# Sums of the input kept in DRAM, and weight sums moved between stages, in a two-layer trunk kernel

## Chip, cores and metric

The kernel runs on one core of a Trainium2 chip. The metric is the device time of one execution in microseconds (us), as the median of several runs. The engines are named as in the profile: PE (TensorE matmul), PEld (its weight loads), DVE (VectorE), ACT (ScalarE), POOL (GpSimd) and SP (SyncE, which here only issues transfers).

## The reference

One sequence of 512 tokens with 2048 channels passes two layers. In the first, `x @ w_in` gives q, k, v, a gate, `z` (1024 columns) and the inputs of a state-space scan. Attention and scan outputs are gated, the scan's by silu(z), concatenated and sent through a first output projection. The second is a pooling mixer: two projections `v` and `g`, causal window means, a small map per group, then `y @ w_out`, the second output projection. Each layer ends in `layer_norm(alpha * x + mixer(x))`.

```python
y = y.reshape(bsz, s, SSM_WIDTH) * jax.nn.silu(z.astype(F32))
...
return jnp.concatenate([y_att, y_ssm], axis=-1) @ w_out     # layer 1
...
return y @ w_out                                            # layer 2
```

## The kernel before

**Products.** All of it is fp32, as three fp32r matmuls per product (`mm3`, lines 105 to 107): each operand is cast to a high part on ACT (line 115) and the rest is taken on DVE (line 116); `split` does both. Weights come in units of 128x1024 (512 KB): `unit` loads one through SP's queue (line 122) into `raw`, and splits it into `hi` and `lo`; each of these three has three buffers. Units are scheduled ahead of other work.

**Winograd-like products.** z and the two output projections are made as 2x2 block products with seven multiplications in place of eight. They need sums of blocks of the activations and sums of blocks of the weights. For z the activation blocks are quarters of x: x1, x2 are the two halves of the channels, H0 and H1 the two halves of the tokens. z needs z1 = x1H1 - x2H1, z2 = z1 - x1H0, z3 = x1H0 - x1H1, z4 = z2 + x2H0. In the kernel before they are made in z's stage: `x_tile` loads 128x256 pieces of x from DRAM (line 511), DVE subtracts and adds piece by piece (lines 521, 535, 536, 538, 546), and each piece is split. The seven products are Yz, Vz (raw x), Wz, then Zz with z1, Yz with z2, Zz with z4, Yz with z3; each is 48 matmuls of 512 columns. The results go through `z_gate` into y.

**Weight sums.** `presum` makes the sums of weight blocks by DMA alone: it loads a block into an SBUF tile, loads others on top with an accumulating transfer, and writes the results t1 to t4 to DRAM, where `unit` fetches them later (`raw<-t`). All its transfers are issued on POOL's queue. One call is a "unit of sums" here: six loads and four writes, in seven steps separated by `yield`. z needs 4 units of sums (`wz`), the first output projection 8 (`wo1`), the second 8 (`wo2`).

**Lanes.** Side work is traced by generators in lanes. Each `mm3` ticks every lane by its nominal time (0.64 for 512 columns), and a lane traces its next step when the amount it yielded has passed. The two lanes `sums2` hold the units of sums, every second unit each; the pace was 7.0 per step. Lanes only set the order of the program: on the chip POOL takes its instructions in order as fast as their own waits let it. From the first `power` on (a small POOL operation that waits for DVE, line 230), `back` puts every transfer of the sums behind the last `power` traced. The pre tiles `pre0`, `pre30`, `pre1`, `pre31` in the pool `keep` are reused, after the lanes are flushed, by the tiles `sr` of the first output projection (line 748).

**Layer 2.** Four groups g of 512 channels: v blocks, g blocks, group map, and `yr[g]` written by ACT (line 960). A residual lane writes x1 to DRAM through POOL (line 905), and after group 0 POOL issues three transfers into `out` (line 965). The prefetch `xq` (line 979) waits on POOL for the last g block.

Of the kernel before, what the change touches and what calls it, by code (L numbers as in the profile page):

```python
# [8 lines left out]
F32 = mybir.dt.float32  # L9
# [17 lines left out]
GROUPS = (346, 346, 348)  # L27
WINDOWS = (2, 4, 8, 16)
NEG = -3.0e38
PACE = 7.0  # L30
AHEAD = 1000


# [22 lines left out]
class Lane:  # L56


    def __init__(self):
        self.gens, self.wait = [], 0.0  # L60

    def push(self, gen):
        if not self.gens:
# [7 lines left out]
            self.gens.pop(0)  # L71

    def tick(self, us):
        self.wait -= us
        while self.gens and self.wait <= 0:
            self.step()
# [6 lines left out]
def ts(j):  # L83
    return slice(j * P, (j + 1) * P)
# [3 lines left out]
def hybrid_trunk(ctx: ExitStack, tc: tile.TileContext, xT, xtok, wa, wg, wz, wo1, wo2, prm, con, lnp, out, dbg=None):  # L88
# [25 lines left out]
    def split(hi, lo, src):  # L114
        nc.scalar.copy(hi, src)  # L115
        nc.vector.tensor_tensor(lo, src, hi.bitcast(F32), ALU.subtract)  # L116
# [80 lines left out]
    def pair(tag):  # L197
        if tag == "sc":
            b = bank2("pZ2")
            return [b[:, 0], b[:, 1]]  # L200
        return [bank(tag, "pY" if tag == "mm" else "pZ") for _ in range(2)]
# [34 lines left out]
            else:  # L236
                nc.gpsimd.dma_start(dst, src)  # L237

    def presum(w, tsum, cp, ch, pool, n, after=None):

        def to(n, t):
            d = tsum[n, cp, ch] = dram.tile([P, 1024], F32, name=f"t{n}_{cp}{ch}")
            back(d, t)

        t = pool.tile([P, 1024], F32, tag=f"pre{n}", name="pre")
        t3 = pool.tile([P, 1024], F32, tag=f"pre3{n}", name="pre3")
        if after is not None:

            nc.gpsimd.tensor_copy(t[:, :1], after)
            nc.gpsimd.tensor_copy(t3[:, :1], after)  # L250
        back(t, wsrc(w, 0, 0, cp, ch))
        back(t3, wsrc(w, 0, 1, cp, ch))
        yield PACE
        back(t, wsrc(w, 0, 1, cp, ch), True)
        back(t3, wsrc(w, 1, 1, cp, ch), True)
        yield PACE
        to(1, t)
        to(3, t3)
        yield PACE
        back(t, wsrc(w, 1, 1, cp, ch), True)  # L260
        yield PACE
        to(2, t)
        yield PACE
        back(t, wsrc(w, 1, 0, cp, ch), True)
        yield PACE
        to(4, t)
        yield PACE


    with ExitStack() as l1:  # L270
# [14 lines left out]
        with ExitStack() as sd:  # L285
# [44 lines left out]
                            mm3(pts[i], hi[:, c], lo[:, c], xh[k], xl[k], k == 0, k == KT - 1)  # L330
            with tc.issue_after(last.ins):
                parameters()
            v = keep.tile([P, NT, 1024], F32, tag="v", name="v")
            y = keep.tile([P, NT, 1024], F32, tag="y", name="y")
            for i in range(4):
                conv_silu(bc[i], pts[i], 8 + i)
            bT, cT = bc[:2], bc[2:]
            btok = [sp.tile([P, 3, P], F32, name=f"btok{g}") for g in range(2)]
            cbm = [sp.tile([P, NT, P], F32, name=f"cbm{g}") for g in range(2)]
# [13 lines left out]
                    yield 3.0  # L353

            lane.push(bc_steps())
            for w, tsum, n in ((wz, tsz, 4), (wo1, ts1, 8), (wo2, ts2, 8)):
                for i in range(n):
                    sums2[i % 2].push(presum(w, tsum, i // 4, i % 4, keep, i % 2,
                                             bc[0][:, :1] if w is wz and i < 2 else None))


# [126 lines left out]
            def z_gate(t, j, c, th):  # L488
# [3 lines left out]
                yz = y[:, t, j * 512:(j + 1) * 512]  # L492
                nc.vector.tensor_tensor(yz, yz, th, ALU.mult)

            Yz, Vz = pair("mm"), pair("mm")
            for ch in range(4):
                prod(Yz, xblock(0, H0), unit(wsrc(wz, 0, 0, 0, ch)), ch, True, False)
# [4 lines left out]
        with tc.tile_pool(name="zs", bufs=1) as zq:  # L502
            def zsum(name):
                hi, lo = (zq.tile([P, 8, 256], F32R, tag=f"{name}{p}", name=f"{name}{p}") for p in "hl")
                return [hi[:, u] for u in range(8)], [lo[:, u] for u in range(8)]

            def x_tile(i, k, c):

                t = zq.tile([P, 256], F32, tag=f"x{i}", name=f"x{i}", bufs=2 + (i == 0))
                o = k % 2 * T + c.start  # L510
                nc.sync.dma_start(t, xT[k // 2 + 4 * (i % 2)][:, o:o + 256])
                return t

            def z_th():
                return zq.tile([P, T], F32, tag="zth", name="zth")

            Wz = pair("sc")
            z1, z2, z4 = zsum("z1"), zsum("z2"), zsum("z4")
            for k in range(8):
                a, b = x_tile(0, k, H1), x_tile(1, k, H1)  # L520
                nc.vector.tensor_tensor(a, a, b, ALU.subtract)
                split(z1[0][k], z1[1][k], a)
            for i in range(2):
                c = zq.tile([P, T], F32, tag="zc", name="zc")
                nc.scalar.copy(c, Yz[i])
                nc.vector.tensor_tensor(c, c, Vz[i], ALU.add)
                z_gate(i, 0, c, z_th())
            for ch in range(4):
                prod(Wz, xblock(8, H1), unit(tsz[4, 0, ch]), ch, True, True)
            Zz = pair("mm")  # L530
            for ch in range(4):
                prod(Zz, z1, unit(tsz[1, 0, ch]), ch, True, False)
            for k in range(8):
                d, e = x_tile(2, k, H0), x_tile(3, k, H0)
                nc.vector.tensor_tensor(d, z1[0][k], d, ALU.subtract)
                nc.vector.tensor_tensor(d, d, z1[1][k], ALU.add)
                split(z2[0][k], z2[1][k], d)
                nc.vector.tensor_tensor(e, e, d, ALU.add)
                split(z4[0][k], z4[1][k], e)
            z3 = zsum("z1")  # L540
            c22 = [zq.tile([P, T], F32, tag=f"c22{i}", name=f"c22{i}") for i in range(2)]
            for i in range(2):
                nc.scalar.copy(c22[i], Zz[i])
            for k in range(8):
                a, d = x_tile(0, k, H1), x_tile(2, k, H0)
                nc.vector.tensor_tensor(a, d, a, ALU.subtract)
                split(z3[0][k], z3[1][k], a)
            for ch in range(4):
                prod(Yz, z2, unit(tsz[2, 0, ch]), ch, False, False)
            for ch in range(4):  # L550
                prod(Zz, z4, unit(wsrc(wz, 1, 1, 0, ch)), ch, False, True)

            for i in range(2):
                c = zq.tile([P, T], F32, tag="zc", name="zc")
                nc.scalar.copy(c, Zz[i])
                nc.vector.tensor_tensor(c, c, Yz[i], ALU.subtract)
                z_gate(i, 1, c, z_th())
            for ch in range(4):
                prod(Yz, z3, unit(tsz[3, 0, ch]), ch, False, True)
            for i in range(2):  # L560
                c = zq.tile([P, T], F32, tag="zc", name="zc")
                nc.scalar.copy(c, Wz[i])
                nc.vector.tensor_tensor(c, c, Yz[i], ALU.add)
                z_gate(2 + i, 0, c, z_th())
                nc.vector.tensor_tensor(c22[i], c22[i], Yz[i], ALU.subtract)
                z_gate(2 + i, 1, c22[i], z_th())

        at = l1.enter_context(tc.tile_pool(name="att1", bufs=1))
        a2s = ExitStack()
# [292 lines left out]
    with ExitStack() as l2:  # L862
# [27 lines left out]
        with ExitStack() as mix:  # L890
# [18 lines left out]
            for g, w in enumerate(WINDOWS):  # L909
# [20 lines left out]
                if g == 0:  # L930
                    for c in range(4):
                        vblock(v0[:, c], vu[c], 256, T)
                        pool_block(c, v0[:, c], 0)
                    for c in range(4):
                        gblock(gts[:, c], gu[c], 0, T)
                else:
                    vu = [next_units(2) for _ in range(4)]
                    gu = [next_units(2) for _ in range(4)]
                    gts = lp.tile([P, 4, T], F32, tag="h2", name="gt")
                    for c in range(4):  # L940
                        vp = p2.tile([P, T + 16], F32, tag="vp", name="vp")
                        nc.vector.memset(vp[:, :16], 0.0)
                        vblock(vp[:, 16:], vu[c], 0, T)
                        pool_block(c, vp, 16)
                    for c in range(4):
                        gblock(gts[:, c], gu[c], 0, T)
                yr.append(lp.tile([P, 2, 2, T], F32, tag=("h0", "l0", "h1", "l1")[g], name=f"yr{g}"))
                for u in range(2):
                    hi, lo = unit(next_units(1)[0])
# [11 lines left out]
                if g == 0:  # L961
                    lane.flush()
                    with tc.issue_after(spill[-1].ins):
                        for t in (0, 2, 3):
                            nc.gpsimd.dma_start(out[0, ts(t)], lnp[1, 1].partition_broadcast(P))
                    a11 = (oc.tile([P, 8, 256], F32R, tag="xp0", name="a11h"), oc.tile([P, 8, 256], F32R, tag="xp1", name="a11l"))
                    s1 = (oc.tile([P, 8, 256], F32R, tag="xp2", name="s1h"), oc.tile([P, 8, 256], F32R, tag="xp3", name="s1l"))
                    sraw = lp.tile([P, 8, 256], F32, tag="l2", name="sraw")
# [214 lines left out]
```

## Time and profile before

| | |
|---|---|
| median of 3 runs | 1426.27 us (1425.15 to 1428.51) |
| the profiled execution | 1426.02 us, span 1424.3 us |
| PE busy | 1386.2 us (97%) |
| PEld busy | 1161.0 us (82%) |
| DVE busy | 878.3 us (62%) |
| ACT busy | 594.4 us (42%) |
| POOL busy | 186.2 us (13%) |
| DMA | 302.74 MB, mean 213 GB/s |

PE busy time is modelled from pipelined matmuls, so a busy PE is not PE at its peak. The granted clock is given as a share of 2.4 GHz.

### The profile page before, as it was taken

The numbers are of one execution on the slowest core, as the hardware profiler recorded it, in microseconds if no ns is written. First come the engines' busy times: TensorE is split into PE (matmuls) and PEld (weight loads), VectorE is DVE, ScalarE is ACT, GpSimd is POOL, SyncE is SP. The second block draws the span as 40 slices with busy tenths as digits, with TensorE's granted clock in tenths as the row PEclk, the third lists the DMA queues.
The fourth block names the chain that finished last, engine by engine and source line by source line (L and its number), as shares of the span: only waits on it lengthen the run. The fifth ranks groups of instructions, "written<-read, shape, count | busy, mean of one in ns | idle before, by whom it ended". The sixth has DMA issues, their size and how long they took to land.

```text
span 1424.3 us, 17633 instructions
## 1 busy us (share of the span) xinstructions
PE 1386.2 (97%) x6653; PEld 1161.0 (82%) x6653; DVE 878.3 (62%) x1311; ACT 594.4 (42%) x984; POOL 186.2 (13%) x281
## 2 busy tenths in 40 slices
PE   9999999978999999999899999999999999999996
PEld 7988899855788888888688889988888888888875
DVE  6656754667755555555687798865445346476777
ACT  5232433434653444444454466423232232344443
POOL 0122222210133222222000000210000000100003
PEclk9999999999999999999999999999999999999998
DMA  7699999996699888879586555783323333466776
GB/s 270 171 311 303 282 279 288 312 306 206 200 291 285 253 247 240 234 239 252 149 271 220 190 175 160 221 285 101 104 89 104 91 102 91 148 223 189 245 246 130
DMA packets 92710, 302.74 MB, mean 213 GB/s; under 512 B 10576, under 2 KB 16848, under 8 KB 92240
## 3 DMA queue, kind: packets, MB, share of 16 engines
q1 hardware_dynamic: 58464, 179.96, 38.5%
q0 software_dynamic: 34160, 121.65, 31.7%
q8 instruction: 52, 0.85, 0.2%
q14 instruction: 34, 0.28, 0.1%
HBM read 251.23 MB, written 53.48 MB: 214 GB/s over the span
## 4 chain that ended last, share of the span: by engine, by line
PE 88%; DVE 4%; DMA 4%; issue 2%; ACT 1%; POOL 1%; DVEq 0%; SPq 0%; ACTq 0%; POOLq 0%
PE pg L106 6%; PE pg L105 6%; PE pg L107 6%; PE pY L105 5%; PE pY L106 4%; PE pY L107 4%; PE pv L106 4%; PE pv L107 4%; PE pv L105 4%; PE pZ L105 3%; PE pZ L106 3%; PE pZ L107 3%; PE pxs L105 2%; PE pxs L107 2%; PE pxs L106 2%; PE pq L107 2%
## 5 line engine op out<-in xcount | busy, mean ns | idle before, releaser
L116 DVE TENSOR_TENSOR lo<-raw,hi 128x1024 fp32r<-128x1024 f32 (+3 forms) x314 | 373.4, 1190 | 347.1 <-ACT hi L115 345.0
L115 ACT CAST hi<-raw 128x1024 fp32r<-128x1024 f32 (+3 forms) x314 | 321.7, 1025 | 546.1 <-PE pY L107 85.2
L105 PE MATMUL pv<-x1h,hi 128*128 128x512 f32 (+1 forms) x320 | 110.9, 347 | 0.0
L106 PE MATMUL pv<-x1l,hi 128*128 128x512 f32 (+1 forms) x320 | 110.9, 347 | 0.0
L107 PE MATMUL pv<-x1h,lo 128*128 128x512 f32 (+1 forms) x320 | 110.7, 347 | 0.0
L105 PE MATMUL pg<-x1h,hi 128*128 128x512 f32 x256 | 99.6, 389 | 0.0
L106 PE MATMUL pg<-x1l,hi 128*128 128x512 f32 x256 | 99.6, 389 | 0.0
L107 PE MATMUL pg<-x1h,lo 128*128 128x512 f32 x256 | 99.6, 389 | 0.0
L237 POOL DMA_DIRECT2D t<-pre x80 | 45.4, 568 | 209.6 <-DMA pre<-in_wo 162.4
L235 POOL DMA_DIRECT2D pre<-in_wo x64 | 56.7, 949 | 79.7 <-DMA t<-pre 50.2
L106 PEld LDWEIGHTS pv<-x1l,hi 128*128 128x128 f32 x320 | 60.5, 189 | 7.7
L105 PEld LDWEIGHTS pv<-x1h,hi 128*128 128x128 f32 x320 | 60.4, 189 | 7.6
L107 PEld LDWEIGHTS pv<-x1h,lo 128*128 128x128 f32 x320 | 60.4, 189 | 7.4
L105 PE MATMUL pg<-hi,xh 128*128 128x346 f32 (+1 forms) x192 | 63.2, 330 | 0.0
L106 PE MATMUL pg<-lo,xh 128*128 128x346 f32 (+1 forms) x192 | 61.8, 322 | 0.0
L107 PE MATMUL pg<-hi,xl 128*128 128x346 f32 (+1 forms) x192 | 61.5, 320 | 0.0
L648 ACT ACTIVATE pm<-psc,st 128x128 f32<-128x128 f32 (+3 forms) x64 | 33.2, 524 | 64.2 <-DVE st L645 64.2
L105 PEld LDWEIGHTS pg<-x1h,hi 128*128 128x128 f32 x256 | 48.1, 188 | 10.0
L106 PEld LDWEIGHTS pg<-x1l,hi 128*128 128x128 f32 x256 | 48.1, 188 | 10.0
L107 PEld LDWEIGHTS pg<-x1h,lo 128*128 128x128 f32 x256 | 48.0, 188 | 9.9
L105 PE MATMUL pgt<-xh,hi 128*128 128x512 f32 x128 | 51.9, 405 | 0.0
L105 PE MATMUL pxs<-xh,hi 128*128 128x512 f32 x128 | 51.6, 403 | 0.0
(363 smaller groups left out, 3288.7 us busy)
## 6 DMA issues: line engine op xcount, KB each, us to landing
raw<-in_wa SPq DMA_DIRECT2D x150, 512.0 KB, 4.0
pre<-in_wo POOLq DMA_DIRECT2D x96, 512.0 KB, 7.7
t<-pre POOLq DMA_DIRECT2D x80, 512.0 KB, 6.4
raw<-t SPq DMA_DIRECT2D x80, 512.0 KB, 4.3
raw<-in_wo SPq DMA_DIRECT2D x48, 512.0 KB, 3.7
pre<-in_wz POOLq DMA_DIRECT2D x24, 512.0 KB, 8.7
raw<-in_wz SPq DMA_DIRECT2D x12, 512.0 KB, 5.8
x<-in_xT SPq DMA_DIRECT2D x48, 128.0 KB, 3.9
```

Source lines behind the costliest of these rows:

```text
L105: nc.tensor.matmul(o, sh, mh, start=start, stop=False, skip_group_check=more)
L106: nc.tensor.matmul(o, sh, ml, start=False, stop=False, skip_group_check=more)
L107: nc.tensor.matmul(o, sl, mh, start=False, stop=stop, skip_group_check=more)
L115: nc.scalar.copy(hi, src)
L116: nc.vector.tensor_tensor(lo, src, hi.bitcast(F32), ALU.subtract)
L235: nc.gpsimd.dma_start(dst, src, accum_op=ALU.add)
L237: nc.gpsimd.dma_start(dst, src)
L648: nc.scalar.activation(pm[:, m, :ke], pt[:, m, :ke], AF.Exp, bias=st[:, 0, i, m:m + 1], scale=1.0, accum_out=st[:, 1, i, m:m + 1])
```

## The change

1. In the first stage, where x lies in SBUF as raw tiles (tags `v` and `y`), four DVE operations of 128x2048 make z1, z3, z2 and z4 in place (`keep_sum`), and POOL writes each (1 MB) to DRAM.
2. In z's stage `fill` loads each sum back in two pieces of 128x1024 (512 KB, two buffers `zo`) through SP and splits them. The 48 loads of x pieces and the 40 DVE operations on them are gone.
3. The two lanes of weight sums are switched off (`off`) from the start of Yz to the end of z's stage.
4. The pace is 8.0 per step for `wo1` and `wo2` in layer 1; of the 8 units of `wo2` only 2 stay in layer 1. The other 6 are pushed after group 0 of layer 2, at pace 10.0, in tiles with the tags of `yr[2]` and `yr[3]` (`h1`, `l1`), behind the last write of x1 on POOL, and flushed before `yr[2]` is made.

```diff
     def tick(self, us):
+        if self.off:
+            return
         self.wait -= us
...
-    def presum(w, tsum, cp, ch, pool, n, after=None):
+    def presum(w, tsum, cp, ch, stage, pace, after=None):
...
-        t = pool.tile([P, 1024], F32, tag=f"pre{n}", name="pre")
-        t3 = pool.tile([P, 1024], F32, tag=f"pre3{n}", name="pre3")
+        t, t3 = stage()
...
+            x1, x2 = (t.rearrange("p u (j c) -> p (u j) c", j=2) for t in xr)
+            zsd = {}
+
+            def keep_sum(n, o, a, b, op):
+                nc.vector.tensor_tensor(o, a, b, op)
+                zsd[n] = dram.tile([P, 8, 256], F32, name=f"zs{n}")
+                nc.gpsimd.dma_start(zsd[n], o)
+
+            keep_sum(1, x2[:, :, H1], x1[:, :, H1], x2[:, :, H1], ALU.subtract)
+            keep_sum(3, x1[:, :, H1], x1[:, :, H0], x1[:, :, H1], ALU.subtract)
+            keep_sum(2, x1[:, :, H0], x2[:, :, H1], x1[:, :, H0], ALU.subtract)
+            keep_sum(4, x2[:, :, H0], x1[:, :, H0], x2[:, :, H0], ALU.add)
...
-            for w, tsum, n in ((wz, tsz, 4), (wo1, ts1, 8), (wo2, ts2, 8)):
+            for w, tsum, n, pace in ((wz, tsz, 4, 7.0), (wo1, ts1, 8, 8.0), (wo2, ts2, 2, 8.0)):
...
+            for l in sums2:
+                l.off = True
             Yz, Vz = pair("mm"), pair("mm")
...
+            def fill(dst, n):
+
+                for q in (slice(0, 4), slice(4, 8)):
+                    o = zq.tile([P, 4, 256], F32, tag="zo", name="zo", bufs=2)
+                    nc.sync.dma_start(o, zsd[n][:, q])
+                    split(dst[2][:, q], dst[3][:, q], o)
...
-            for k in range(8):
-                a, b = x_tile(0, k, H1), x_tile(1, k, H1)
-                nc.vector.tensor_tensor(a, a, b, ALU.subtract)
-                split(z1[0][k], z1[1][k], a)
+            fill(z1, 1)
...
+            for l in sums2:
+                l.off = False
...
+                if g == 2:
+                    for l in sums2:
+                        l.flush()
                 yr.append(lp.tile([P, 2, 2, T], F32, tag=("h0", "l0", "h1", "l1")[g], name=f"yr{g}"))
...
+                    def stage2(n):
+
+                        def get():
+                            a = lp.tile([P, 2, 1024], F32, tag=("h1", "l1")[n], name="pre2")
+                            return a[:, 0], a[:, 1]
+                        return get
+
+                    rank[:] = [spill[-1]]
+                    for i in range(2, 8):
+                        sums2[i % 2].push(presum(wo2, ts2, i // 4, i % 4, stage2(i % 2), 10.0))
```

## Rows read from the trace of the kernel before

**Rows 1.** Busy time by stretch: PE, PEld, DVE, ACT, POOL, clock, DMA share, GB/s.
```profile
302.04:380.33 78.29, 63.66 (x241) 46.66 (x240) 60.42 (x111) 37.39 (x65) 1.76 (x2) 0.93 0.73 228
675.00:700.00 25.00, 19.05 (x78) 15.49 (x77) 15.30 (x31) 11.68 (x27) 1.96 (x3) 0.86 0.56 148
725.00:750.00 25.00, 25.00 (x112) 20.71 (x111) 23.72 (x33) 12.87 (x15) 0.00 (x0) 1.00 0.94 324
```

**Rows 2.** Timeline of z's stage, engines PE and SP: start, duration, instruction.
```profile
302.04 0.39 PE L105 MATMUL pY<-hi,z1h 128*128 128x512 f32 x1
371.49 0.39 PE L105 MATMUL pk<-xh,hi 128*128 128x512 f32 x1
380.33 0.39 PE L105 MATMUL pq<-xh,hi 128*128 128x512 f32 x1
294.41 1.97 SPq L511 DMA_DIRECT2D x<-in_xT  x4
```

**Rows 3.** Waits of PE from 286 to 340 us: total us, times, longest.
```profile
PE pY L105 <- ACT z1h L115: 4.8, 1, 4.8
PE pY L105 <- ACT z2h L115: 4.4, 2, 3.5
PE pY L107 <- DVE z1l L116: 1.6, 1, 1.6
```

**Rows 4.** Groups of instructions from 300 to 375 us: busy, mean ns, idle before.
```profile
L116 DVE TENSOR_TENSOR lo<-raw,hi 128x1024 fp32r<-128x1024 f32 x19 | 23.1, 1222 | 6.6 <-ACT hi L115 6.6
L105 PE MATMUL pY<-hi,z1h 128*128 128x512 f32 x32 | 14.5, 452 | 8.0 <-ACT z1h L115 5.1 <-DVE zc L556 1.7 <-DVE zc L526 1.2
L115 ACT CAST z1h<-x 128x256 fp32r<-128x256 f32 x16 | 6.3, 403 | 12.0 <-DVE x L521 10.3 <-DVE x L546 1.8
L521 DVE TENSOR_TENSOR x<-x,x 128x256 f32<-128x256 f32 x8 | 3.4, 421 | 7.8 <-DMA x<-in_xT 7.8
```

**Rows 5.** Waits of PE from 660 to 740 us.
```profile
PE pat L661 <- DVE pm L653: 3.9, 1, 3.9
PE psc L642 <- ACT pm L648: 2.1, 1, 2.1
```

**Rows 6.** Timeline from 668 to 697 us, engines DVE, POOL and PE.
```profile
685.78 0.69 DVE L748 TENSOR_TENSOR sr<-yTs,yTa 128x512 f32<-128x512 f32 x1 [6.42 <-DMA t<-pre]
668.54 1.04 POOL L230 TENSOR_TENSOR ss<-ss,nhalf 128x4 f32<-128x4 f32 x1 [7.65 <-DVE ss L698]
692.52 0.63 PE L105 MATMUL pY<-hi,a11h 128*128 128x512 f32 x1
696.36 0.60 PE L105 MATMUL pY<-hi,a11h 128*128 128x512 f32 x1
```

**Rows 7.** Busy time in the first stage and in a stretch of weight sums, columns as rows 1.
```profile
31.00:46.00 15.00, 15.00 (x68) 12.43 (x67) 3.30 (x6) 2.80 (x4) 0.00 (x0) 1.00 0.24 71
75.00:275.00 200.00, 200.00 (x1063) 175.69 (x1062) 119.00 (x158) 78.50 (x144) 51.74 (x77) 1.00 1.01 299
```

**Rows 8.** DMA issues over the whole span: count, size, median us from issue to landing.
```profile
raw<-t SPq DMA_DIRECT2D x80, 512.0 KB, 4.3
pre<-in_wz POOLq DMA_DIRECT2D x24, 512.0 KB, 8.7
```

**Rows 9.** POOL's issues of the writes t1 to t4, by stretch: busy (count).
```profile
53.00:306.70 253.70, 21.77 (x38) 1.00 1.01 296
306.70:384.50 77.80, 0.00 (x0) 0.93 0.69 211
384.50:686.00 301.50, 23.62 (x42) 1.00 0.89 255
```

**Rows 10.** Timeline: first write of v, last issues before and write of yr[2] in layer 2.
```profile
80.51 0.44 ACT L366 COPY v<-pg 128x330 f32<-128x330 f32 x1
943.63 1.57 POOL L965 DMA_DIRECT2D out<-in_lnp  x3
1150.46 0.72 ACT L960 ACTIVATE yr<-y,osc 128x512 f32<-128x512 f32 x1 [2.19 <-DVE y L958]
```

More of the change, by code (lines that the diff above doesn't have):

```diff
@@ L29 @@
 NEG = -3.0e38
-PACE = 7.0
 AHEAD = 1000
@@ L59, in __init__ @@
     def __init__(self):
-        self.gens, self.wait = [], 0.0
+        self.gens, self.wait, self.off = [], 0.0, False
     def push(self, gen):
@@ L252, in presum @@
         back(t3, wsrc(w, 0, 1, cp, ch))
-        yield PACE
+        yield pace
         back(t, wsrc(w, 0, 1, cp, ch), True)
         back(t3, wsrc(w, 1, 1, cp, ch), True)
-        yield PACE
+        yield pace
         to(1, t)
         to(3, t3)
-        yield PACE
+        yield pace
         back(t, wsrc(w, 1, 1, cp, ch), True)
-        yield PACE
+        yield pace
         to(2, t)
-        yield PACE
+        yield pace
         back(t, wsrc(w, 1, 0, cp, ch), True)
-        yield PACE
+        yield pace
         to(4, t)
-        yield PACE
+        yield pace
     with ExitStack() as l1:
@@ L332, in hybrid_trunk @@
                 parameters()
+            for i in range(4):
+                conv_silu(bc[i], pts[i], 8 + i)
+            x1, x2 = (t.rearrange("p u (j c) -> p (u j) c", j=2) for t in xr)
[8 more added lines that the diff above has]
+            keep_sum(4, x2[:, :, H0], x1[:, :, H0], x2[:, :, H0], ALU.add)
             v = keep.tile([P, NT, 1024], F32, tag="v", name="v")
             y = keep.tile([P, NT, 1024], F32, tag="y", name="y")
-            for i in range(4):
-                conv_silu(bc[i], pts[i], 8 + i)
             bT, cT = bc[:2], bc[2:]
@@ L355, in hybrid_trunk, with stage1 @@
             lane.push(bc_steps())
-            for w, tsum, n in ((wz, tsz, 4), (wo1, ts1, 8), (wo2, ts2, 8)):
+            def stage1(n):
+                return lambda: [keep.tile([P, 1024], F32, tag=f"pre{i}{n}", name="pre") for i in ("", 3)]
+            for w, tsum, n, pace in ((wz, tsz, 4, 7.0), (wo1, ts1, 8, 8.0), (wo2, ts2, 2, 8.0)):
                 for i in range(n):
-                    sums2[i % 2].push(presum(w, tsum, i // 4, i % 4, keep, i % 2,
+                    sums2[i % 2].push(presum(w, tsum, i // 4, i % 4, stage1(i % 2), pace,
                                              bc[0][:, :1] if w is wz and i < 2 else None))
@@ L504, in zsum @@
                 hi, lo = (zq.tile([P, 8, 256], F32R, tag=f"{name}{p}", name=f"{name}{p}") for p in "hl")
[L505 to L512, printed above, removed]
+                return [hi[:, u] for u in range(8)], [lo[:, u] for u in range(8)], hi, lo
+            def fill(dst, n):
[3 more added lines that the diff above has]
+                    split(dst[2][:, q], dst[3][:, q], o)
             def z_th():
@@ L532, in hybrid_trunk @@
                 prod(Zz, z1, unit(tsz[1, 0, ch]), ch, True, False)
[L533 to L539, printed above, removed]
+            fill(z2, 2)
+            fill(z4, 4)
             z3 = zsum("z1")
@@ L543, in hybrid_trunk @@
                 nc.scalar.copy(c22[i], Zz[i])
[L544 to L547, printed above, removed]
+            fill(z3, 3)
             for ch in range(4):
```

## The prediction

> **What bounds the kernel now.** I read the busy time in stretches of 25 us first, then the waits of PE in the stretches where it wasn't full, then the timeline around them. The reader should see that PE is full in almost every stretch and is short of work in two places only: z's stage and the turn from attention to the first output projection. Everything else that the change touches can only matter if it takes PE's work away.
>
> *z's stage.* Zz's first matmul starts at 302.04 and the first q block at 380.33 [rows 2]. Between them lie four products and one k block, 5 x 48 = 240 matmuls of 512 columns, as the count of x241 in that stretch says [rows 1]. At full clock one such matmul follows another every (380.33 - 371.49) / 39 = 0.2267 us (39 starts lie between these two rows) [rows 2]. The work is thus 240 x 0.2267 = 54.4 us and took 78.29: 23.9 us are lost. The idle time is 78.29 - 63.66 = 14.6 us, and the rest, 9.3 us, is lost to the clock: at a mean of 0.93, 2 x 0.07 x 78.29 = 11 us of the stretch lay at 1.2 GHz, busy or idle [rows 1].
>
> The Trainium skill ("Perfetto Trace Analysis", Identifying the Most-Contended Engine) says that the matmul's busy share is a poor measure of headroom and the share of weight loads a good one. By the busy column the prize would be 14.6 us and the forecast near 1404; by the weight loads it is 78.29 - 46.66 / (20.71 / 25) = 22.0 us and the forecast near 1399, a full stretch being 725 to 750 [rows 1]. The count of matmuls agrees with the rule, and I go on with the count.
>
> What ended the idle time is the chain behind the x pieces: PE waits for the casts z1h and z2h and for z1l [rows 3], the cast z1h waits 10.3 us for the subtraction of line 521, and that one 7.8 us for the loads of x [rows 4]. These loads can't begin before 294.41 [rows 2], when the scan's tiles, whose place they take, are free. So at 302.04 PE arrives at operands that come in 128 KB pieces, through four small DVE operations each.
>
> *The turn.* PE idles 3.9 us for DVE's pm and 2.1 us for ACT's pm [rows 5]. Both are late because DVE, in order, stands for 6.42 us in front of sr, which takes the place of the weight sums' tiles and waits for the last write of those sums [rows 6]. After it the clock is at 1.2 GHz: from 692.52 to 696.36 nine matmuls start 0.427 us apart in place of 0.2267 [rows 6], about ten in all, 2.0 us. Together 8.0 us.
>
> **The change, part by part.**
>
> *Early sums.* Four DVE operations of 2048 columns; the nearest is 1.22 us for 1024 columns [rows 4], so 2.4 each, 9.8 us in all. Their input has landed before 31 us, and from 31 to 46 DVE is busy 3.30 of 15 us while PE is full [rows 7], so 11.7 us are free. A split may be late by one such operation, 2.4 us; PE then still has two units in hand, each worth 24 matmuls. Cost 0, and even without that cover 2.4 us. The four stores of 1 MB stand in POOL's queue ahead of the first units of sums. The nearest price is at most 8.7 us for 512 KB [rows 8], so 17.4 for one; they overlap, and v's place is first written at 80.51 [rows 10], more than 30 us after the sums. Cost 0; if DVE made the sums only after the convolutions, some 30 us later, the stores would still be in time or late by a few us (upper end 5).
>
> *The fills.* The two loads of z1 go out at 294.4 and 294.8. Landing takes 4.3 us at the median and 8.7 at the worst group [rows 8]. I take 4.3, as the pause removes POOL's transfers that ran until 306 [rows 9]: first half at 298.7, cast by about 299.8, rest by 301.0, which is before 302.04. The second half is needed 24 matmuls later, at 307.5. At 8.7 the rest is there at about 305.5: 3 us of idle time and a fall of the clock, 6 us in all (upper end). z2, z4 and z3 are each needed a product, 10.9 us, after the one before, and two loads with two splits take about 4.3 + 2 x 2.3 = 9: hidden. On DVE, 40 operations and 32 small splits of 0.42 us go (30.2 us) and 8 of 1.22 come (9.8), so 60.42 busy [rows 1] become 40 of the 57 us that remain. DVE is busy 23.72 of 25 from 725 to 750 with PE full [rows 1], so that is no bound.
>
> *What stays in z's stage:* the wait of 1.7 us for line 556 [rows 4], which separates two products on one accumulator and isn't touched; with its ramps 2.6. So 23.9 - 2.6 = 21.3 us come back, at least 15 with the upper end above.
>
> *The pause and the pace.* POOL isn't paced on the chip: it issued 38 writes, 9.5 units of sums, in 253.7 us (26.7 each) and then nothing until 384.5, when the first power of the attention stage let it go on; then 10.5 units in 301.5 us (28.7 each) [rows 9]. Up to Yz the lanes are ticked by 165 us (by the rule of line 109, three groups of 64 products of about 346 columns, 27.7 each, and eight blocks of 16 products of 512 columns, 10.24 each). With 14 steps of 7.0 and then steps of 8.0 that makes 23 steps per lane, 3.3 units, 6.6 in all. They are over at about 53 + 6.6 x 26.7 = 229 and don't meet z's loads. All four units for z are among them. 7.4 units remain for attention. Per lane they are 26 steps of 8.0, 208 of attention's 246 us of ticks. In the kernel before, 36 steps of 7.0 remained, 252: the last were traced behind the power of head 6, at 668.54 [rows 6], and that is why they were late. Head h's power is traced at about 45 + 30.7 h, so 208 lies behind head 5's (199) and ahead of head 6's (230): one head earlier, about 39 us. By DMA they need 7.4 x 28.7 = 212 us from 364, so they are not bound by it. The sums end near 620 and sr comes near 658. The wait of 6.42 us goes and with it 8.0 us, between 5 (the last head's own chain shows through) and 10. If the cover of 38 us were gone, it would return one to one.
>
> *Six units in layer 2.* 60 transfers are issued on POOL after 943.63 + 1.57 = 945 [rows 10], some 916 with the gains. A pair of units, one in each lane, takes 53.4 to 57.4 us [rows 9], three pairs at most 172, to 1088. yr[2], which takes the place of one lane's tiles, is written at 1150.46 [rows 10], then 1121. Cover 33 us. The weight loads share the DMA with them: from 75 to 275 they did so too, at a share of 1.01, with PE full 200 of 200 us [rows 7]. Cost 0. The Trainium skill ("DMA: Bandwidth & Descriptors", Issuing engines are not separate DMA queues) speaks against it: transfers of all queues run on the same engines and interleave. The trace agrees that they slow each other, but not PE: the row from 75 to 275 is that case.
>
> *Sum:* 21.3 + 8.0 = 29.3 us. The profiled execution took 1426.02, 0.25 below the median of 1426.27, so it stands for the runs: 1426.0 - 29.3 = 1396.7, say 1397. If both losses went wholly (23.9 + 10), 1392.
>
> **Rivals.**
> 1. *The first fill is late* (0.14). For it: the loads still begin only at 294.4, and ACT and DVE take the splits in an order fixed at build time, so a gate operation may stand behind a cast that waits. Against: 4 MB land in 8 loads in place of 6 MB in 48, and only the first two are urgent. 6 us more, up to 9: 1403, to 1406.
> 2. *The wait in front of sr stays* (0.09). For it: POOL's order is fixed by the scheduler, and the last steps may again fall behind head 6's power. Against: 22 units of ticks between the two. 8 us more: 1405.
> 3. *ACT and DVE can't keep up in the shorter z stage* (0.06). The gates and splits that were spread over 78 us must pass in 57. DVE at 40 of 57 speaks against it. Half of 21.3 would be lost: 1408.
> 4. *Slower: yr[2] waits for the sums in layer 2* (0.05). ACT stands in front of line 960, casts of units stop, and after two units (10.9 us) PE does. It decides when a pair of units takes over (1121 - 916) / 3 = 68 us; the kernel is slower by over 0.2% once the delay eats 29.3 + 10.9 + 3, at 83 us a pair, against 57.4 in the slowest stretch: 1430 or more. For it: POOL's queue is in order, and one late transfer holds both lanes.
> 5. *The change doesn't do what it says* (0.04): both waits move to the next link and nothing is left: 1426.
>
> **How the numbers follow.** 0.2% of 1426 is 2.9 us, about what a measurement of this kernel can tell from no change. The forecast has 0.62, with a range of its own of 1392 to 1402. The range from 1391 to 1409 takes in the rivals 1 to 3 and leaves out 4 and 5 and the tails. Faster: 0.62 + 0.14 + 0.09 + 0.06 = 0.91; the same 0.04 and slower 0.05.
>
> **What would show it.** Right: from Wz's end to the first q block about 57 us with the clock at 1.0; no DVE wait for x loads; POOL idle from about 230 until attention; no wait of DVE in front of sr; in layer 2 some 60 issues of POOL between about 916 and 1088 with PE full. Wrong: PE waits for z1h again, a wait of sr for a write of sums, ACT's line 960 waiting for a transfer, or PE below full in the first 80 us because the early sums or their stores stand in the way.

## The result and the profile after

The kernel after the change took 1394.41 us (median of 4 runs, 1393.37 to 1395.49), the kernel before 1427.19 beside it on the same chip (4 runs, 1425.15 to 1428.51): a ratio of 0.9772 [0.9755, 0.9789]. The forecast was 1397, with a range from 1391 to 1409. The span of the profiled execution fell from 1424.3 to 1393.5 us.

I set four places of PE's work beside each other, each the start of the first matmul of its kind: z1's product, the q block, the first output projection's product with `a12h`, and the end of the span. The first table of differences is all that is needed to see where the time came from.

| us | z1 | q | a12h | end | z1 to q | q to a12h | a12h to end |
|---|---|---|---|---|---|---|---|
| before | 302.04 | 380.33 | 721.07 | 1424.3 | 78.29 | 340.74 | 703.2 |
| after | 301.21 | 359.21 | 690.48 | 1393.5 | 58.00 | 331.27 | 703.0 |

Of the 30.8 us of span, 20.3 are z's stage, 9.5 are attention with the turn behind it, 0.8 lie ahead of z1, and the rest of the kernel is as long as it was.

*z's stage.* Busy time by stretch of the kernel after, columns as in [rows 1], the first row z's stage from z1 to q:

```profile
301.21:359.21 58.00, 56.04 (x241) 44.59 (x240) 44.08 (x48) 32.54 (x40) 0.00 (x0) 1.00 0.69 227
675.00:700.00 25.00, 25.00 (x123) 20.74 (x121) 17.32 (x25) 14.54 (x28) 1.01 (x1) 1.00 0.60 200
31.00:46.00 15.00, 15.00 (x68) 12.43 (x67) 9.46 (x8) 2.80 (x4) 2.57 (x3) 1.00 0.98 333
75.00:275.00 200.00, 200.00 (x1065) 175.64 (x1065) 119.17 (x159) 78.84 (x144) 38.79 (x57) 1.00 0.85 248
914.00:1085.00 171.00, 171.00 (x756) 141.62 (x755) 80.64 (x115) 52.96 (x66) 40.66 (x61) 1.00 1.01 303
```

The same 241 matmuls now pass in 58.00 us, the clock is at 1.00 in place of 0.93, and DVE does 48 operations in place of 111. In the turn (675 to 700) PE is full at full clock. The three rows below these are the places that had to pay: the early sums (31 to 46), the lanes up to Yz (75 to 275) and the sums in layer 2 (914 to 1085). PE is full in each.

The waits of PE that are left from 296 to 360 us, and the one that is left from there to the first output projection; then the timeline of SP and ACT around the first fill:

```profile
PE pY L107 <- DVE lo L117: 1.2, 3, 0.8
PE pY L106 <- DVE zc L564: 0.7, 1, 0.7
PE pyt L600 <- DVE y L594: 1.0, 1, 1.0
```

```profile
293.65 1.06 SPq L530 DMA_DIRECT2D zo<-zs  x2
297.79 1.05 ACT L116 CAST z1h<-zo 128x1024 fp32r<-128x1024 f32 x1 [0.77 <-DMA zo<-zs]
```

No wait for z1h or z2h is left of those in [rows 3]. The cast of z1's first half starts 3.4 us before PE's first matmul of that product (301.21).

*The turn.* Timeline of the kernel after, engines POOL and DVE, at the end of the sums:

```profile
607.59 1.03 POOL L231 TENSOR_TENSOR ss<-ss,nhalf 128x4 f32<-128x4 f32 x1 [15.27 <-DVE ss L708]
608.60 1.18 POOL L238 DMA_DIRECT2D t<-pre  x2
608.66 0.69 DVE L711 TENSOR_TENSOR o<-pav,ss 128x512 f32<-128x512 f32 x1 [1.22 <-POOL ss L231]
612.48 0.69 DVE L758 TENSOR_TENSOR sr<-yTs,yTa 128x512 f32<-128x512 f32 x1 [3.13 <-DMA t<-pre]
616.51 0.17 DVE L654 MEMSET psc<- 64x128 f32 x1
```

The wait in front of sr is still there. It is 3.13 us long in place of 6.42 [rows 6], it stands 73 us earlier, and no wait of PE follows it. The rows around it show where it stands: behind `o`, one head's attention output, and ahead of DVE's first operation on `psc`, the scores of the next head.

*The pause and layer 2.* Timeline of POOL and, last row, ACT:

```profile
217.96 0.87 POOL L236 DMA_DIRECT2D pre<-in_wo  x1 [1.94 <-DMA pre<-in_wo]
363.05 1.04 POOL L231 TENSOR_TENSOR rs<-rs,nhalf 128x4 f32<-128x4 f32 x1 [144.22 <-DVE rs L590]
914.31 0.55 POOL L238 DMA_DIRECT2D pre<-in_wo  x1
1082.87 0.55 POOL L238 DMA_DIRECT2D t<-pre  x1 [3.24 <-DMA pre<-in_wo]
1119.86 0.72 ACT L973 ACTIVATE yr<-y,osc 128x512 f32<-128x512 f32 x1 [2.19 <-DVE y L971]
```

POOL issues nothing between 218.8 and 363. In layer 2 the three pairs of units run from 914.3 to 1083, some 56 us a pair, and `yr[2]` comes 37 us later, waiting for DVE and not for a transfer.

### The profile page after: what moved, and what is told of

Same layout as the page of the kernel before. It is cut to its first block, busy times and chain, and to the rows that moved or that the text cites. A ratio compares the mean times of both kernels' runs of the same rounds, so it can differ in the third digit from the quotient of the medians.

```text
span 1393.5 us, 17492 instructions
## 1 busy us (share of the span) xinstructions
PE 1374.1 (99%) x6653; PEld 1155.7 (83%) x6653; DVE 871.0 (63%) x1251; ACT 590.7 (42%) x960; POOL 189.1 (14%) x285
## 4 chain that ended last, share of the span: by engine, by line
PE 90%; DVE 3%; DMA 3%; ACT 1%; issue 1%; POOL 1%; DVEq 0%; SPq 0%; ACTq 0%; POOLq 0%
PE pg L107 6%; PE pg L106 6%; PE pg L108 6%; PE pv L107 4%; PE pv L108 4%; PE pv L106 4%; PE pY L107 4%; PE pY L108 4%; PE pY L106 4%; PE pZ L106 3%; PE pZ L107 3%; PE pZ L108 3%; PE pgt L108 2%; PE pk L107 2%; PE pxs L106 2%; PE pgt L106 2%
```

## The experiments

Twelve kernels ran. The letters in the expectations stand for the theories that each of them names. The medians of before, run on the same chip, were 1426.72 (first four), 1426.30 (next four) and 1425.12 us (last four).

| run | us (median) | ratio to before | z1 to q | q to a12h | a12h to end |
|---|---|---|---|---|---|
| early_only | 1407.17 | 0.987 [0.9852, 0.9889] | 61.56 | 339.81 | 702.8 |
| move_only | 1421.14 | 0.9959 [0.9939, 0.998] | 73.67 | 340.45 | 702.8 |
| no_pause | 1406.00 | 0.9859 [0.9841, 0.9878] | 59.22 | 340.43 | 703.7 |
| fill_small | 1395.64 | 0.9787 [0.9771, 0.9803] | 58.05 | 331.24 | 703.4 |
| pause_only | 1465.99 | 1.0279 [1.0261, 1.0296] | 71.55 | 333.53 | 757.0 |
| no_move | 1479.86 | 1.0372 [1.0356, 1.0388] | 56.14 | 331.27 | 788.1 |
| move_late | 1395.36 | 0.9779 [0.9764, 0.9793] | 57.10 | 331.25 | 703.1 |
| early_unused | 1427.62 | 1.0003 [0.9991, 1.0015] | 81.25 | 339.72 | 703.3 |
| before_sr3 | 1424.14 | 0.9998 [0.9982, 1.0013] | 77.75 | 339.02 | 703.7 |
| early_sr3 | 1407.37 | 0.9875 [0.9855, 0.9894] | 63.84 | 337.63 | 702.2 |
| no_pause_sr3 | 1407.91 | 0.9875 [0.9853, 0.9896] | 58.64 | 340.48 | 703.6 |
| move_late2 | 1437.21 | 1.0084 [1.0062, 1.0107] | 58.31 | 331.24 | 743.6 |

**The early sums alone** (early_only: the kernel after without the pause, with all 8 units of `wo2` in layer 1 at a pace of 7.0).

```diff
-            for l in sums2:
-                l.off = True
...
-            for w, tsum, n, pace in ((wz, tsz, 4, 7.0), (wo1, ts1, 8, 8.0), (wo2, ts2, 2, 8.0)):
+            for w, tsum, n, pace in ((wz, tsz, 4, 7.0), (wo1, ts1, 8, 7.0), (wo2, ts2, 8, 7.0)):
...
-                    for i in range(2, 8):
-                        sums2[i % 2].push(presum(wo2, ts2, i // 4, i % 4, stage2(i % 2), 10.0))
```

> The kernel before with the early sums and the fills alone: all 20 units of weight sums stay in layer 1 at pace 7.0, without the pause. Theory A (z's loss is the chain of x loads and small DVE operations; the two gains are separate): the time from z1's first matmul to the first q block falls from 78.3 to 58 to 63 us, the wait before sr stays, 1403 to 1411 us. Theory B (z gains because the pause keeps the weight sums' transfers away from its loads): the fills collide with POOL's transfers until some 306 us, z's stretch stays above 68 us, 1415 us or more.

Measured 1407.17, as expected. z's stage falls to 61.56 us, and the turn stays: PE waits 4.2 us for pm by DVE and 1.9 for pm by ACT, beside 3.9 and 2.1 in [rows 5]; pm is a block of a head's scores behind the exponential, which PE transposes next.

**The early sums made and stored, but not used** (early_unused: before, with the four DVE operations and four stores; z's stage still subtracts pieces of x).

```diff
+            keep_sum(1, x2[:, :, H1], x1[:, :, H1], x2[:, :, H1], ALU.subtract)
...
+            keep_sum(4, x2[:, :, H0], x1[:, :, H0], x2[:, :, H0], ALU.add)
```

> The kernel before with the four early sums made and stored to DRAM by POOL, but read by nothing: z's stage is as before. Theory A (9.8 us of DVE work and 4 MB of stores are hidden): 1425 to 1429 us, PE full from 25 to 250 us. Rival: the work delays splits or the first weight sums and costs 3 us or more: 1430 us or more.

Measured 1427.62, no difference from before. The price of the first stage is nothing, as PE's 15.00 of 15.00 us from 31 to 46 says too.

**The fills in small pieces** (fill_small: 128x256 with eight buffers, as in the kernel before, but of finished sums).

```diff
-                for q in (slice(0, 4), slice(4, 8)):
-                    o = zq.tile([P, 4, 256], F32, tag="zo", name="zo", bufs=2)
+                for q in (slice(u, u + 1) for u in range(8)):
+                    o = zq.tile([P, 1, 256], F32, tag="zo", name="zo", bufs=8)
```

> The changed kernel with each fill in 8 pieces of 128x256 (32 loads of 128 KB, eight buffers, small splits) in place of 2 of 128x1024. Theory A (what counted was the operations between load and cast, and that all buffers can be asked for at once): z's stretch 58 to 64 us, 1394 to 1401 us. Theory C (what counted was the size of the pieces, since 128 KB loads and 256-column operations are dear): z's stretch above 68 us, 1405 us or more.

Measured 1395.64, z's stage 58.05. The size of the pieces is not what cost the kernel before its time. What is left are its DVE operations between load and cast, its second load per pair of pieces, and its two or three buffers for each kind of piece, where this run has eight. No run tells these three apart.

**No pause** (no_pause: the kernel after without the two `off` loops).

```diff
-            for l in sums2:
-                l.off = True
...
-            for l in sums2:
-                l.off = False
```

> The changed kernel without the pause; the weight sums go on being traced through z's stage. Theory A: z's stretch is 58 to 62 us and the time 1393 to 1399 us. Theory B: z's stretch goes above 68 us and the time above 1404 us.

Measured 1406.00: theory A missed by 7 us, and the time that B gave came about in another place than B said. z's stage is 59.22 us, 1.2 longer than in the kernel after. The rest of the loss is in attention, 340.43 in place of 331.27. Timeline of POOL and DVE of this run, then the wait of PE:

```profile
493.17 1.03 POOL L231 TENSOR_TENSOR ss<-ss,nhalf 128x4 f32<-128x4 f32 x1 [10.47 <-DVE ss L704]
494.17 1.82 POOL L236 DMA_DIRECT2D pre<-in_wo  x2
505.81 0.69 DVE L651 TENSOR_REDUCE st<-psc 128x2 f32<-128x512 f32 x1
...
517.01 0.55 POOL L238 DMA_DIRECT2D t<-pre  x1 [2.01 <-DMA pre<-in_wo]
518.16 0.69 DVE L754 TENSOR_TENSOR sr<-yTs,yTa 128x512 f32<-128x512 f32 x1 [11.65 <-DMA t<-pre]
519.22 0.48 DVE L659 SCALAR_TENSOR_TENSOR pm<-pm,st 128x256 f32<-128x256 f32 x1
```

```profile
PE pat L667 <- DVE pm L659: 6.5, 1, 6.5
```

The sums end 92 us earlier than in the kernel after, and yet DVE stands 11.65 us in front of sr. So sr does not lie at a fixed place that the sums must beat: its place in DVE's order goes along with the sums.

**The move alone** (move_only: before, with part 4 of the change).

```diff
-            for w, tsum, n in ((wz, tsz, 4), (wo1, ts1, 8), (wo2, ts2, 8)):
+            for w, tsum, n, pace in ((wz, tsz, 4, 7.0), (wo1, ts1, 8, 8.0), (wo2, ts2, 2, 8.0)):
...
+                    for i in range(2, 8):
+                        sums2[i % 2].push(presum(wo2, ts2, i // 4, i % 4, stage2(i % 2), 10.0))
```

> The kernel before with the six units of sums moved to layer 2 and the new pace, without early sums and without the pause. Theory A: the turn's loss goes (9 to 10 us), z's stretch stays at 76 to 80 us, 1416 to 1420 us. Theory B: the same here unless the slower pace alone thins the transfers in z's stage; then z's stretch is below 72 us and the time below 1412 us.

Measured 1421.14, close above the range, but not for the reason given. The turn's loss is whole (340.45): sr stands 11.08 us at 530, and PE waits 5.9 us for pm there. What was gained is 4.6 us of z's stage, where the last transfer of sums goes out at 290.67 in place of 306.

**The pause alone, and the pause without the move** (pause_only: before, with the two `off` loops; no_move: the kernel after, with 8 units of `wo2` in layer 1).

```diff
-            for w, tsum, n, pace in ((wz, tsz, 4, 7.0), (wo1, ts1, 8, 8.0), (wo2, ts2, 2, 8.0)):
+            for w, tsum, n, pace in ((wz, tsz, 4, 7.0), (wo1, ts1, 8, 8.0), (wo2, ts2, 8, 8.0)):
...
-                    for i in range(2, 8):
-                        sums2[i % 2].push(presum(wo2, ts2, i // 4, i % 4, stage2(i % 2), 10.0))
```

> The kernel before with the pause alone: x pieces in z's stage as before, all 20 units in layer 1 at pace 7.0. Theory A: z's stretch is 72 to 78 us, since its chain of small operations stays; the sums that are left for attention, some 13 units at 28.7 us, end near 760 us, where sr needs them near 680, and PE loses most of these 80 us: 1480 to 1510 us. Theory B: z's stretch falls to 60 to 66 us, and the turn loses the same: 1465 to 1495 us. The two are told apart by z's stretch.

> The changed kernel with all 8 units of the second projection in layer 1 (pace 8.0, pause kept). Theory A (the wait for the last sums comes back one to one once their cover is gone): 13.4 units at 28.7 us from 363 us end near 748; DVE stands in front of sr for some 90 us and PE, with two units in hand, loses about 80: 1460 to 1485 us. Rival: the scheduler puts sr so that DVE has other work first and PE loses under 20 us: below 1415 us.

Measured 1465.99 and 1479.86, both slower than before. For pause_only z's stage, which was to tell the two theories apart, is at 71.55, by A's side, while the time lies 14 us below A's range. no_move came into theory A's range, with the sums ending near 797 in place of 748 and a wait of DVE half as long as expected. Attention is free of sr's wait (333.53 and 331.27), but the sums are late for the first output projection itself. Waits of PE in no_move from 690 to 1030 us, and POOL's last write of a sum:

```profile
PE pZ L106 <- ACT s1h L116: 71.6, 2, 69.9
```

```profile
796.69 0.55 POOL L238 DMA_DIRECT2D t<-pre  x1 [4.86 <-DMA pre<-in_wo]
```

DVE stands 45.2 us in front of sr, and ACT's cast of it is what PE waits for.

**The turn by another tile** (before_sr3, early_sr3, no_pause_sr3: sr takes the tiles `pre30` and `pre31`, whose last write comes a few steps earlier in a unit).

```diff
-        sr = [keep.tile([P, 2, 2, 256], F32, tag=f"pre{n}", name="sr")[:, i] for n in range(2) for i in range(2)]
+        sr = [keep.tile([P, 2, 2, 256], F32, tag=f"pre3{n}", name="sr")[:, i] for n in range(2) for i in range(2)]
```

> The kernel before with sr put in the tiles of t3 (pre30, pre31), which a unit of sums frees four steps before those of t (pre0, pre1); nothing else. Theory D (the wait at the turn is the lag of the sums' last writes behind the schedule that put sr there, whatever the number of units): DVE's wait for t<-pre in front of sr goes or falls below 3 us, the time from the first q block to the first a12 product falls from 340.7 to 331 to 333 us, 1416 to 1420 us. Rival F: sr is put earlier with the tile and waits as long as before: 1424 to 1429 us.

> The kernel before with early sums and fills, all 20 units in layer 1, no pause, and sr in the tiles of t3. Theory D: both losses are gone without pause and without move, 1395 to 1400 us. Rival F: as with early sums alone, 1405 to 1411 us.

> The changed kernel without the pause and with sr in the tiles of t3. Theory D (the pause only shortened the lag in front of sr): 1393 to 1398 us, as the changed kernel. Rival E (the pause is needed because it keeps POOL's transfers away from z's stage and the attention): above 1402 us.

Measured 1424.14, 1407.37 and 1407.91: no gain in any. Theory D fell. Rival F's times came in the first two, and rival E's in the third, but not in both of the places that E named: z's stage is 58.64, and the loss is in attention (340.48). POOL and DVE in before_sr3:

```profile
627.91 1.03 POOL L230 TENSOR_TENSOR ss<-ss,nhalf 128x4 f32<-128x4 f32 x1 [10.68 <-DVE ss L698]
...
653.27 0.53 POOL L237 DMA_DIRECT2D t<-pre  x1 [2.90 <-DMA pre<-in_wo]
656.55 0.69 DVE L748 TENSOR_TENSOR sr<-yTs,yTa 128x512 f32<-128x512 f32 x1 [7.70 <-DMA t<-pre]
```

With the tile free earlier, sr is put earlier by 29 us and waits 7.70 us there. PE waits 5.1 us for pm behind it.

**The six units later** (move_late: pushed after group 1; move_late2: as that, and held by a small POOL copy that reads `yr[1]`; the last three lines below are in move_late2 alone).

```diff
+                if g == 1:
+
                     def stage2(n):
...
-                    rank[:] = [spill[-1]]
+                    rk = lp.tile([P, 1], F32, tag="rk", name="rk")
+                    rank[:] = [nc.gpsimd.tensor_copy(rk, yr[1][:, 1, 1, :1])]
```

> The changed kernel with the six units pushed after group 1 of layer 2 in place of group 0, flushed before yr[2] as now. Theory A (yr[2] waits for the sums; this was the rival on the slower side): in the changed kernel the six units took from 914 to about 1088 us; begun near 1031 they end near 1205, ACT stands in front of yr[2] from 1120, and PE loses about 75 us: 1455 to 1480 us. Rival: units go faster when begun later, or the casts pass ACT's wait: below 1420 us.

> The changed kernel with the six units of layer 2 held behind a POOL copy that reads yr[1] (written near 1030 us), so that they can't begin before. In the run in which they were only traced later they still began near 910 us. Now begun near 1031 they last some 170 us, to 1200; ACT stands in front of yr[2] from 1120, PE loses 65 to 80 us: 1455 to 1478 us. Rival: PE is covered by other work: below 1420 us.

move_late measured 1395.36, about the same as the kernel after, where 1455 to 1480 were expected; the rival's time came, but not for its reasons: its first transfer of these units goes out at 913.99, in place of 914.31. Tracing them later doesn't hold them, since nothing on the chip does. In move_late2 the copy does. Timeline of POOL and ACT, and the wait of PE from 1000 to 1300:

```profile
1031.11 0.48 POOL L993 COPY rk<-yr 128x1 f32<-128x1 f32 x1 [116.77 <-ACT yr L973]
...
1172.78 0.55 POOL L238 DMA_DIRECT2D t<-pre  x1 [1.72 <-DMA pre<-in_wo]
1175.94 1.95 ACT L973 ACTIVATE yr<-y,osc 128x512 f32<-128x512 f32 x3 [47.74 <-DMA t<-pre]
```

```profile
PE pv L106 <- ACT hi L116: 37.9, 1, 37.9
```

It took 1437.21, 43 us more than the kernel after and slower than before by 0.84% [0.62, 1.07]: this is the wait of rival 4, brought about by the copy. The time is 18 us below the least that I expected. The last write of the sums went out at 1179.66.

## Why the prediction was right, and where it was not

*z's stage: right.* The sum gave 21.3 us, the trace 20.3. By the count of matmuls 58.00 - 54.4 = 3.6 us are still lost, not 2.6. Of the 2.6, 1.7 were the wait for line 556, which now measures 0.7 (line 564), and no row gives the 0.9 for ramps. Of the 3.6, 1.96 are idle time of PE, and the other 1.6 I have not taken apart. The fills were as costed: issued at 293.65, first half landed by 297.79 where I said 298.7. DVE had 44.08 us of work in 58.00 where I said 40 of 57, and that was no bound. early_only, early_unused and fill_small together show the cause: finished sums alone bring 16.7 us in this stage (78.29 to 61.56; 13.9 between before_sr3 and early_sr3), making them costs nothing, and small pieces of them are as good. The remaining 3.6 us (61.56 to 58.00) come with less traffic of the weight sums: 2.3 by the move and the pace (no_pause, 59.22), 1.2 by the pause. Single profiles of one stage differ by some us, as 61.56 and 63.84 of early_only and early_sr3 do, so this last split is rough: among the five kernels that have both fills and pause the stage takes 56.14 to 58.31, a spread wider than the 1.2.

The Trainium skill ("Perfetto Trace Analysis", Identifying the Most-Contended Engine) prefers weight loads to matmul busy time as a measure of headroom. The trace after agrees: by weight loads 58.00 - 44.59 / (20.71 / 25) = 4.2 us are left, near the count's 3.6, while the busy column says 2.0. Of the prediction's two forecasts by these columns, 1399 takes off the 2.6 us that stay and 1404 does not; taken alike, the busy column gives 1406.

*The early sums: right.* Four operations at 2.28 to 2.29 us each, where 2.4 was the estimate, between 26.56 and 39.7; PE full.

*The pause: right in its place, wrong in its worth.* POOL's last issue before z was at 217.96 (estimate 229), and the units were over before z's loads. But the loads hardly need it (1.2 us). Its worth is in the turn: no_pause and the kernel after differ by 11.6 us (1406.00 and 1394.41), and the profiles show 9.2 us of difference between q and a12h.

*The turn: size right, mechanism wrong.* This is the step that failed: "The sums end near 620 and sr comes near 658. The wait of 6.42 us goes". The sums did end near 610, one head earlier as worked out, but sr came at 612.48 and waited 3.13 us: "a wait of sr for a write of sums", the prediction's own sign of being wrong. The cover of 38 us never was there; rival 2 was right that the wait stays, and wrong that it then costs 8 us. The runs put sr behind the release of its tile wherever that is:

| run | last `power` | last write issued | transfers from that `power` to that write | DVE waits for sr | PE waits for pm |
|---|---|---|---|---|---|
| before | 668.54 | 684.63 | 6 | 6.42 | 6.0 |
| move_only | 505.63 | 528.92 | 8 | 11.08 | 5.9 |
| no_pause | 493.17 | 517.01 | 8 | 11.65 | 6.5 |
| before_sr3 (`pre3` tiles) | 627.91 | 653.27 | 12 | 7.70 | 5.1 |
| after | 607.59 | 608.60 (x2) | 2 | 3.13 | 0 |

The order of DVE is fixed when the kernel is built, and in these runs it puts sr close to the release of the tile. In the first four runs several links of load and write, each waiting for the one before, are still to come when the last `power` releases POOL; they take 16 to 25 us on the chip, and DVE arrives 6 to 12 us before they are done. In the kernel after only two writes are left, both loaded long before. DVE arrives 3.1 us early, and PE does not wait.

What DVE's wait holds up differs too. In the first four runs sr stands inside a head's scores: in no_pause, between the reduction of a block's scores (505.81) and the `pm` of that block (519.22), for which PE waits. In the kernel after it stands between two heads. Successive powers of the heads are 39.4 us apart; behind the last `power` of the table the next comes 48.55, 48.14, 48.26 and 46.82 us later in the first four runs, and 39.41 in the kernel after. So the loss, 7 to 9 us, grows neither with DVE's wait (6.42 to 11.65) nor with the number of transfers (6 to 12). Few links left and a place between two heads came together in the kernel after, and no run tells which of them saved PE; that cause stays open. Shown is that an earlier end of the sums (no_pause, move_only) and an earlier release of the tile (the three sr3 runs) do not remove the loss. That the change cut just there came from where its lanes happened to stop, not from the one head of distance that I worked out: by the prediction's own ticks 208 against 199 leave one step per lane behind head 5's power, which is the two writes, where 252 against 230 left about three, the six transfers. Nothing aimed at that, so this part of the forecast came out by luck.

The size was 9.5 us for 8.0. The idle part was right (6.0 of PE's waits). The clock's part was taken too small: PE was busy 333.62 us in this stretch before and 330.28 after, with the same 1634 matmuls, so the lower clock had cost 3.3 us and not 2.0. I had counted ten slow matmuls in one row and not the whole stretch. Busy time of the stretch in the kernel before, then after, columns as in [rows 1]:

```profile
380.33:721.07 340.74, 333.62 (x1634) 278.48 (x1632) 186.44 (x330) 159.47 (x370) 79.95 (x112) 0.99 0.83 240
```

```profile
359.21:690.48 331.27, 330.28 (x1634) 276.42 (x1632) 185.89 (x329) 159.12 (x370) 59.53 (x82) 1.00 0.68 199
```

*Layer 2: right.* Start 914.3 (estimate 916), end 1083 (at most 1088), `yr[2]` 1119.86 (1121), cost 0. The cover is 37 us where I said 33, and move_late2 shows what it covers: with a start 117 us later, ACT waits 47.7 us and PE 37.9. The cushion between the two is 9.8 us, near the two units (10.9) of rival 4's sum. Held together, its three pairs took some 50 us each, in place of 56, which may be part of why it cost less than expected.

*The sum.* The move looked like an extra, free but worth little; the runs show that pause and move have to go together. Alone the pause costs 39.7 us (pause_only), with the early sums and without the move it costs even more (no_move), and the move alone brings 5.6. Together, on top of the early sums, they bring 12.8 (1407.17 to 1394.41). The pace of 8.0 was not tried by itself: every run with the move has it too.

## What to carry to other kernels

When an in-order engine stands in front of a reused tile, do not assume that an earlier end of the work on that tile removes the stand: the build may move the waiting instruction forward along with it. Look at how much of the chain is still to run behind the last thing that releases it, and at which operations of the same engine stand behind the wait at that place. And before crediting an edit with a gain, run it alone: here the part that seemed decisive for z's loads (the pause) acted in attention, more than 200 us later.

## What the runs showed of the hardware

DMA at a share of 1.01 for 171 us, with 61 POOL instructions in the stretch, took nothing from a full PE: 171.00 of 171.00 us busy, with 756 matmuls of 512 columns, one every 0.226 us. The Trainium skill ("DMA: Bandwidth & Descriptors", Issuing engines are not separate DMA queues) says that transfers of all queues share the engines and interleave; the trace agrees: in that stretch the 512 KB weight loads landed after 6.9 us at the median, and after 3.7 us between 914 and 1085 us of the kernel before, which has no sums there. They still came in time. And a stop reaches further than its own length: behind 6.0 us of waits in the turn of the kernel before, 3.3 us more were lost at the lower clock (a mean of 0.86 from 675 to 700 us, [rows 1]), against the 2.0 that one row had suggested.
